# Sliding-window attention scores as row-tiled float32r products: two heads on the two halves of the array

## The chip, the cores and the metric

The kernel runs on one core of one Trainium2 chip. The metric is the device time of one execution in microseconds (us). Three runs of the kernel before gave a median of 2125.07 us. TensorE (PE in the profile) multiplies, VectorE (DVE) and ScalarE (ACT) do the elementwise work, SyncE (SP) issues nearly all transfers. PEld is TensorE's loading of weights, the operand that stays in the array while the other one streams past.

## The reference, cut to what matters

One decoder layer: a projection, four heads of a gated linear recurrence (HGRN2) beside eight heads of sliding-window attention, an output projection, and a gated MLP. Only the scores of the attention are touched by the change:

```python
# q: 8 heads of 64 features; k, v: 2 heads of 64; blocks of 128 queries read
# their own 128 keys and the 128 before them
scale = 1.0 / math.sqrt(ATT_HD)
scores = jnp.einsum('bnqhgd,bnkhd->bnhgqk', qb, kb) * scale
scores = jnp.where(mask, scores, -jnp.inf)          # causal, window of 128
m = jnp.maximum(jnp.max(scores, axis=-1, keepdims=True), sink)
p = jnp.exp(scores - m)
denom = jnp.sum(p, axis=-1, keepdims=True) + jnp.exp(sink - m)
out = jnp.einsum('bnhgqk,bnkhd->bnqhgd', p / denom, vb)
```

## The kernel before, in words

The 2048 tokens are worked through in two halves of 1024. Each half has a mixing stage (projections, recurrence, attention), then the output projection, the MLP with its seven products for a 2x2 block (Strassen's scheme) and the down projection, which also starts the next half.

Nearly every product is made in parts: a float32 operand is split into a high part rounded to float32r (`fp32r` in the profile) and a low part, the rest. A product is then high·high + high·low + low·high, three float32r matmuls into one bank of PSUM.

In the attention a pair `j` (0 to 3) is one head of the first group of four and one of the second, so that its query tile `qT` has 64 features of the one head in rows 0 to 63 and 64 of the other in rows 64 to 127; the keys `kT` have the two key heads in the same way. `rows(kv)` is the half of the rows that belongs to head `kv` of the pair.

`att_keys` (from line 432) makes the keys' tile `KS`, with a column for each of 2 kinds, 128 carried keys and the half's 1024. For head `kv`, `KS[:, kv]` holds the high part of the 64 features in that head's own rows (line 450) and the low part in the other 64 rows (line 451): 128 rows, both parts stacked.

`attend` (from line 463) runs for each pair. For 512 queries (`g`) and each head, lines 479 to 482 make `qh`, the high part of the queries in both halves of the rows, and `ql`, the low part in both halves, by three ACT copies and one DVE subtraction of 64x512 each. Lines 483 to 493 make the scores of two blocks of 128 queries in one PSUM bank `psc`: for each block the matmul with weights `qh` (128 rows, 128 queries) and the moving operand `KS[:, kv]` (128 rows, 256 keys) gives high·high + high·low, the one with `ql` gives low·high + low·low. So two matmuls with all 128 rows give the scores of a head's block: 4 for the two heads of a pair. Over 4 pairs and 16 blocks that is 256. In the first block of the sequence there are only 128 keys. Lines 494 to 502 take the bank to the tile `sc`: an ACT copy of the previous block's half of the scores and a predicated DVE copy of the own block's half.

The banks come from pools of two: `ps("at", ...)` is the pool with which scores (`psc`), transposed probabilities (`ppt`) and attention outputs (`poT`) share two banks; `"hg"` has two for the recurrence, `"mm"` four for the projections.

`ORDER` interleaves the steps of recurrence heads (H) and pairs (A); inside that, a scheduler with its own simulated timeline sets the order of the instructions on each engine when the kernel is built. On PE the score matmuls thus lie in small groups between 128x512 matmuls of the projections (`q`, `g`, `f`, `pop`, `pvv` from line 222 or 750 to 752) and those of the recurrence. PE executes in order.

Some of the recurrence's matmuls and the attention's output have fewer than 128 columns of weights and are put in column tiles: `plev` and `pdiag` (lines 586, 637, 643) in 32 columns, `poT` (line 541) and a last `plev` (line 649) in 64. The profile writes the shape of the weights ahead of the operand: `128*128` is a matmul with all rows and columns, `128*32` and `128*64` are column tiles. A float32 matmul, as in these, stands there as two records, a float32r one as one.

Of the kernel before, what the change touches and what calls it, by code (L numbers as in the profile page):

```python
# [8 lines left out]
F32 = mybir.dt.float32  # L9
F32R = mybir.dt.float32r  # L10
# [3 lines left out]
ALU = mybir.AluOpType  # L14
# [3 lines left out]
P = 128  # L18
# [35 lines left out]
def hymba_layer(ctx: ExitStack, tc: tile.TileContext, a: dict, out: bass.AP):  # L54
    nc = tc.nc
# [18 lines left out]
    def ps(kind, name):  # L74
        return spaces[kind].tile([P, 512], F32, tag=kind, name=name)
# [3 lines left out]
    def halves():  # L79
        return [(b, slice(b * 512, (b + 1) * 512)) for b in range(NB)]  # L80
# [243 lines left out]
    def slot(name):  # L324
        return hp.tile([P, HALF], F32, tag="m", name=name, bufs=KT)
# [103 lines left out]
    def rows(kv):  # L429
        return slice(kv * HD, (kv + 1) * HD)  # L430

    def att_keys(hf, kv, invb, p):

        KS = p.tile([P, 2, P + HALF], F32R, name="KS")
        V = p.tile([P, 1 + TT, P], F32, name="V")
        if hf:
            nc.vector.tensor_copy(KS[:, :, 0:P], kc)  # L440
            nc.vector.tensor_copy(V[:, 0], vc)
        kT, vT = [p.tile([P, HALF], F32, tag="t4", name=n, bufs=2) for n in ("kT", "vT")]
        for jj, dst in ((ATT_J, kT), (ATT_J + 1, vT)):
            o = kv[jj - ATT_J]
            for b, bs in halves():
                nc.vector.tensor_tensor(dst[:, bs], o[b], invb[:, bs], op=ALU.mult)
                nc.scalar.activation(dst[:, bs], dst[:, bs], AF.Identity, bias=C.battn[:, jj:jj + 1])
        for kv in range(2):
            r, other = rows(kv), rows(1 - kv)
            nc.scalar.copy(KS[r, kv, P:], kT[r])  # L450
            nc.vector.tensor_tensor(KS[other, kv, P:], kT[r], KS[r, kv, P:].bitcast(F32), op=ALU.subtract)
        for b in range(NB):
            pv = ps("at", "pv")
            for i in range(4):
                t0 = (b * 4 + i) * P
                nc.tensor.transpose(pv[:, i * P:(i + 1) * P], vT[:, t0:t0 + P], ident)
            nc.scalar.copy(V[:, 1 + 4 * b:5 + 4 * b].rearrange("p a b -> p (a b)"), pv)
        if hf + 1 < NH:
            nc.vector.tensor_copy(kc, KS[:, :, HALF:HALF + P])
            nc.vector.tensor_copy(vc, V[:, TT])  # L460
        return KS, V

    def attend(hf, j, X, invb, KS, V, mix, p):

        o = unit(a["w_att"][j], X, "q")
        qT = slot(f"att{j}")
        for b, bs in halves():
            nc.vector.scalar_tensor_tensor(qT[:, bs], o[b], 0.125, invb[:, bs], op0=ALU.mult, op1=ALU.mult)
            nc.scalar.activation(qT[:, bs], qT[:, bs], AF.Identity, bias=C.bq[:, j:j + 1])
        yield  # L470
        scs = []
        for g in range(NB):
            sc = p.tile([P, 2, 4, P], F32, tag="sc", name="sc", bufs=2)
            gs = slice(g * 512, (g + 1) * 512)
            for kv in range(2):
                r, other = rows(kv), rows(1 - kv)

                qh, ql = [p.tile([P, 512], F32R, tag="pp", name=n, bufs=4) for n in ("qh", "ql")]
                nc.scalar.copy(qh[r], qT[r, gs])
                nc.scalar.copy(qh[other], qT[r, gs])  # L480
                nc.vector.tensor_tensor(ql[r], qT[r, gs], qh[r].bitcast(F32), op=ALU.subtract)
                nc.scalar.copy(ql[other], ql[r].bitcast(F32))
                for i0 in (0, 2):
                    pb = ps("at", "psc")
                    first = hf == 0 and g == 0 and i0 == 0
                    for i in range(2):
                        n = g * 4 + i0 + i
                        w0 = 1 if first and i == 0 else 0
                        o = pb[:, i * 256 + w0 * P:(i + 1) * 256]
                        ks = slice((n + w0) * P, (n + 2) * P)  # L490
                        for t, qx in enumerate((qh, ql)):
                            nc.tensor.matmul(o, qx[:, (i0 + i) * P:(i0 + i + 1) * P], KS[:, kv, ks],
                                             start=t == 0, stop=t == 1)
                    pv = pb.rearrange("p (i w k) -> p i w k", i=2, w=2)
                    dst = sc[:, kv, i0:i0 + 2]
                    if first:
                        nc.vector.memset(dst[:, 0], NEG)
                        nc.scalar.copy(dst[:, 1], pv[:, 1, 0])
                    else:
                        nc.scalar.copy(dst, pv[:, :, 0])  # L500
                    nc.vector.copy_predicated(
                        dst, C.own.bitcast(U32).unsqueeze(1).to_broadcast([P, 2, P]), pv[:, :, 1])
            m = p.tile([P, 2, 4], F32, tag="mx", name="m", bufs=2)
            nc.vector.tensor_reduce(m.rearrange("p a b -> p (a b)"),
                                    sc.rearrange("p a b c -> p (a b) c"), axis=AX.X, op=ALU.max)
            sk = C.sinkb[:, j].unsqueeze(2).to_broadcast([P, 2, 4])
            nc.vector.tensor_tensor(m, m, sk, op=ALU.max)
            es = p.tile([P, 2, 4], F32, tag="es", name="es", bufs=2)
            nc.vector.tensor_tensor(es, sk, m, op=ALU.subtract)
            nc.vector.tensor_scalar(m, m, -1.0, None, op0=ALU.mult)  # L510
            den = p.tile([P, 2, 4], F32, tag="den", name="den", bufs=2)
            for kv in range(2):
                for i in range(4):
                    nc.scalar.activation(sc[:, kv, i], sc[:, kv, i], AF.Exp, bias=m[:, kv, i:i + 1],
                                         accum_out=den[:, kv, i:i + 1])
            nc.scalar.activation(es, es, AF.Exp)
            nc.vector.tensor_tensor(den, den, es, op=ALU.add)
            nc.vector.reciprocal(den, den)
            nc.vector.tensor_tensor(sc, sc, den.unsqueeze(3).to_broadcast([P, 2, 4, P]), op=ALU.mult)
            scs.append(sc)  # L520
        yield
        for g, sc in enumerate(scs):
            pm = []
            for kv in range(2):
                pm.append([p.tile([P, 4, P], F32, tag="pp", name=n, bufs=4) for n in ("po", "pp")])
                pt = ps("at", "ppt")
                for i in range(4):
                    nc.tensor.transpose(pt[:, i * P:(i + 1) * P], sc[:, kv, i], ident)
                ptv = pt.rearrange("p (i q) -> p i q", i=4)
                for dst, mk in zip(pm[kv], (C.ownT, C.prevT)):  # L530
                    nc.vector.tensor_tensor(dst, ptv, mk.unsqueeze(1).to_broadcast([P, 4, P]), op=ALU.mult)
            oT = ps("at", "poT")
            first = None
            for i in (3, 2, 1, 0):
                n = g * 4 + i
                noprev = hf == 0 and n == 0
                for prev in (0,) if noprev else (1, 0):
                    for kv in (1, 0):
                        r = rows(kv)
                        with tc.issue_after(first) if first else ExitStack():  # L540
                            mm = nc.tensor.matmul(oT[r, i * P:(i + 1) * P], V[:, n + 1 - prev, r], pm[kv][prev][:, i],
                                                  start=noprev or prev == 1, stop=prev == 0)
                        first = first or mm.ins
            gs = slice(g * 512, (g + 1) * 512)
            if j < ATT_J - 1:
                nc.scalar.copy(qT[:, gs], oT)
                mix[4 + j] = qT
            else:
                if g == 0:
                    mix[4 + j] = new_x()  # L550
                h, l = mix[4 + j]
                nc.scalar.copy(h[:, gs], oT)
                nc.vector.tensor_tensor(l[:, gs], oT, h[:, gs].bitcast(F32), op=ALU.subtract)
            yield
# [694 lines left out]
    for hf in range(NH):  # L1249
        X, kv, invb, rs, f0 = nxt  # L1250
        with ExitStack() as st:
            p = pool(f"mix{hf}", stack=st, reuse_waits="tile")
            KS, V = att_keys(hf, kv, invb, p)
# [6 lines left out]
            for n, step in enumerate(ORDER.split()):  # L1260
                i = int(step[1:] or 0)
# [16 lines left out]
        with ExitStack() as st:  # L1278
            p = pool(f"ffn{hf}", stack=st, reuse_waits="tile")
            kept, ops, hs, first, last = out_proj(hf, M, p)  # L1280
# [63 lines left out]
```

## Time and profile before

| | |
|---|---|
| median of 3 runs | 2125.07 us (2124.28 to 2125.99) |
| the profiled execution | 2124.22 us |
| its span, first to last instruction | 2122.6 us |
| PE busy | 2108.1 us, 99% of the span |
| DVE, ACT busy | 1624.3 us (77%), 1096.2 us (52%) |
| granted TensorE clock | 1.000 |

A line of the timeline has the start and the duration in us, then engine, line, operation, output<-inputs, the shape of the weights, the shape of the moving operand, and how many such records in a row it merges. Matmuls are pipelined: one record lasts longer than the distance to the next, so the distance from start to start is what a matmul costs in a stream. Scores are made in two stretches, about 114 to 350 us and 1085 to 1400 us of the span.

### The profile page before, as it was taken

What the parts mean: (1) busy time and instruction counts of PE and PEld (TensorE: products, weight loads), DVE (VectorE), ACT (ScalarE), POOL (GpSimd) and SP (SyncE); (2) the same over time, 40 slices, a digit from 0 to 9 for tenths busy, and PEclk for the clock granted to TensorE, in tenths of its full rate; (3) what the DMA queues carried; (4) which work ended last, traced back from release to release, by engine and by line L of the source; (5) the groups of instructions that cost most, each with busy time, mean ns of one, the idle gap of its engine ahead of it and who ended that gap; (6) DMA issues with size and microseconds to landing.
All of it is one profiled execution on the core that took longest, in us unless ns stands there. A gap on an engine that the chain in (4) does not pass through costs nothing.

```text
span 2122.6 us, 29885 instructions
## 1 busy us (share of the span) xinstructions
PE 2108.1 (99%) x11584; PEld 1748.9 (82%) x11584; DVE 1624.3 (77%) x2374; ACT 1096.2 (52%) x1880; POOL 22.3 (1%) x52
## 2 busy tenths in 40 slices
PE   9999999999999999999999999999999999999998
PEld 7888888888888888888888888888888888878888
DVE  7457787898878878775863677868988787887766
ACT  6456575664434444335734476656544444443453
POOL 1000000000000000000000000000000000000000
PEclk9999999999999999999999999999999999999999
DMA  4111111523332325955731010213223223279643
GB/s 160 43 40 43 33 47 47 173 75 101 107 116 85 126 88 190 393 199 168 233 105 52 31 36 31 81 49 142 95 90 124 94 95 119 85 242 372 228 134 134
DMA packets 96475, 255.21 MB, mean 120 GB/s; under 512 B 17355, under 2 KB 19659, under 8 KB 96333
## 3 DMA queue, kind: packets, MB, share of 16 engines
q1 hardware_dynamic: 91076, 251.32, 34.4%
q10 hardware_dynamic: 5256, 1.98, 0.4%
q8 instruction: 91, 1.49, 0.3%
q14 instruction: 52, 0.42, 0.1%
HBM read 195.11 MB, written 57.16 MB: 119 GB/s over the span
## 4 chain that ended last, share of the span: by engine, by line
PE 97%; DVE 1%; ACT 1%; DMA 1%; issue 0%; SPq 0%; DVEq 0%; ACTq 0%
PE pop L222 8%; PE X L933 8%; PE X L934 8%; PE X L935 7%; PE q L222 4%; PE g L222 4%; PE f L222 4%; PE hq L222 4%; PE Y L935 4%; PE Y L933 4%; PE Y L934 4%; PE pdx L1151 3%; PE pdx L1153 3%; PE pdx L1152 3%; PE pdy L1151 3%; PE pdy L1152 3%
## 5 line engine op out<-in xcount | busy, mean ns | idle before, releaser
L758 ACT CAST whi<-raw 128x1024 fp32r<-128x1024 f32 x88 | 92.7, 1053 | 102.9 <-PE X L934 61.1
L933 PE MATMUL X<-T,whi 128*128 128x512 f32 x352 | 137.1, 389 | 0.0
L934 PE MATMUL X<-T,whi 128*128 128x512 f32 x352 | 136.9, 389 | 0.0
L935 PE MATMUL X<-T,wlo 128*128 128x512 f32 x352 | 136.9, 389 | 0.0
L1032 DVE SCALAR_TENSOR_TENSOR y<-ga,cw,y 128x1024 f32<-128x1024 f32 x88 | 112.6, 1281 | 28.4 <-ACT y L1030 28.2
L940 ACT COPY u<-X 128x512 f32<-128x512 f32 x88 | 51.7, 588 | 124.4 <-PE X L935 124.3
L200 ACT CAST whi<-raw 128x1024 fp32r<-128x1024 f32 x57 | 59.5, 1050 | 101.2 <-PE hq L222 33.5
L201 DVE TENSOR_TENSOR wlo<-raw,whi 128x1024 fp32r<-128x1024 f32 x57 | 69.4, 1222 | 54.8 <-ACT whi L200 54.5
L759 DVE TENSOR_TENSOR wlo<-raw,whi 128x1024 fp32r<-128x1024 f32 x88 | 107.4, 1221 | 0.3 <-ACT whi L758 0.3
L222 PE MATMUL pop<-XL,whi 128*128 128x512 f32 x256 | 88.7, 392 | 0.0
L631 ACT COPY G<-QK 128x1024 f32<-128x1024 f32 x48 | 51.4, 1070 | 71.7 <-DVE QK L653 66.5
L222 PE MATMUL pop<-XH,wlo 128*128 128x512 f32 x256 | 88.4, 391 | 0.0
L759 DVE TENSOR_TENSOR xld<-raw,xhd 128x1024 fp32r<-128x1024 f32 x72 | 81.1, 1134 | 9.3 <-ACT xhd L758 9.1
L222 PE MATMUL pop<-XH,whi 128*128 128x512 f32 x256 | 87.9, 394 | 0.0
L758 ACT CAST xhd<-raw 128x1024 fp32r<-128x1024 f32 x72 | 69.6, 978 | 27.1 <-DMA raw<-act0T 7.4
L933 PEld LDWEIGHTS X<-T,whi 128*128 128x128 f32 x352 | 66.1, 188 | 14.1 <-ACT u L940 0.4
L935 PEld LDWEIGHTS X<-T,wlo 128*128 128x128 f32 x352 | 66.1, 188 | 13.8
L934 PEld LDWEIGHTS X<-T,whi 128*128 128x128 f32 x352 | 66.0, 188 | 13.7
L1151 PE MATMUL pdx<-xhd,hid 128*128 128x512 f32 x192 | 74.5, 392 | 1.5 <-ACT xhd L758 0.9
L1152 PE MATMUL pdx<-xld,hid 128*128 128x512 f32 x192 | 74.7, 389 | 0.0
L653 DVE TENSOR_TENSOR QK<-QK,f 128x1024 f32<-128x1024 f32 x56 | 68.6, 1225 | 6.7 <-ACT G L631 5.9
L1153 PE MATMUL pdx<-xhd,lod 128*128 128x512 f32 x192 | 73.7, 389 | 0.0
(394 smaller groups left out, 6329.5 us busy)
## 6 DMA issues: line engine op xcount, KB each, us to landing
wr<-in_w_down SPq DMA_DIRECT2D x90, 512.0 KB, 4.9
raw<-in_w_gate SPq DMA_DIRECT2D x44, 512.0 KB, 3.5
raw<-in_w_up SPq DMA_DIRECT2D x44, 512.0 KB, 3.6
raw<-act0T SPq DMA_DIRECT2D x20, 512.0 KB, 5.0
raw<-act1T SPq DMA_DIRECT2D x20, 512.0 KB, 6.8
act0B<-y SPq DMA_DIRECT2D x33, 256.0 KB, 2.4
act1B<-y SPq DMA_DIRECT2D x33, 256.0 KB, 4.1
raw<-in_w_out SPq DMA_DIRECT2D x16, 512.0 KB, 4.4
```

Source lines behind the costliest of these rows:

```text
L201: nc.vector.tensor_tensor(lo, raw, hi.bitcast(F32), op=ALU.subtract)
L222: marks["unit"] = nc.tensor.matmul(o[b], w, x[:, bs], start=f, stop=l)
L653: done = nc.vector.tensor_tensor(own, own, Fv.rearrange("p b w -> p w b").unsqueeze(3).to_broadcast([P, 2, nb, m]), op=ALU.mult)
L758: return (nc.scalar.copy(h, src), (eng or nc.vector).tensor_tensor(l, src, h.bitcast(F32), op=ALU.subtract))
L759: (eng or nc.vector).tensor_tensor(l, src, h.bitcast(F32), op=ALU.subtract))
L933: nc.tensor.matmul(o, wh[:, ws], xh, start=i == 0 and not more, stop=False, skip_group_check=more)
L934: nc.tensor.matmul(o, wh[:, ws], xl, start=False, stop=False, skip_group_check=more)
L935: r = nc.tensor.matmul(o, wl[:, ws], xh, start=False, stop=i == 3, skip_group_check=more)
L1032: nc.vector.scalar_tensor_tensor(y, g[:, w:w + HALF], C.cw[:, ft, w:w + 1], y, op0=ALU.mult, op1=ALU.add)
L1151: nc.tensor.matmul(o, wh[:, i, c], ah[:, i, cols], start=f, stop=False, skip_group_check=more)
L1152: nc.tensor.matmul(o, wh[:, i, c], al[:, i, cols], start=False, stop=False, skip_group_check=more)
L1153: nc.tensor.matmul(o, wl[:, i, c], ah[:, i, cols], start=False, stop=l, skip_group_check=more)
```

## The change: three products on 64 rows for each head, the heads in turn

`KS` now holds both heads in every column, high parts in `KS[:, 0]` and low parts in `KS[:, 1]`, 64 rows to a head. `qh` and `ql` are the parts of both heads' queries, made by one ACT copy and one DVE subtraction of 128x512. For each block of queries there are three matmuls to a head, `qh`·high, `ql`·high and `qh`·low, each on the 64 rows of that head; in the built program those have a tile of 64 rows and 128 columns, at row 0 for the first head and at row 64 for the second. The code writes the two heads in turn, each into a bank of its own, so that two banks of the pool of two are taken at once. A pair's block has 6 matmuls in place of 4, the whole kernel 384 in place of 256. The product low·low falls away.

```diff
-        for kv in range(2):
-            r, other = rows(kv), rows(1 - kv)
-            nc.scalar.copy(KS[r, kv, P:], kT[r])
-            nc.vector.tensor_tensor(KS[other, kv, P:], kT[r], KS[r, kv, P:].bitcast(F32), op=ALU.subtract)
+        nc.scalar.copy(KS[:, 0, P:], kT)
+        nc.vector.tensor_tensor(KS[:, 1, P:], kT, KS[:, 0, P:].bitcast(F32), op=ALU.subtract)
...
-            for kv in range(2):
-                r, other = rows(kv), rows(1 - kv)
-
-                qh, ql = [p.tile([P, 512], F32R, tag="pp", name=n, bufs=4) for n in ("qh", "ql")]
-                nc.scalar.copy(qh[r], qT[r, gs])
-                nc.scalar.copy(qh[other], qT[r, gs])
-                nc.vector.tensor_tensor(ql[r], qT[r, gs], qh[r].bitcast(F32), op=ALU.subtract)
-                nc.scalar.copy(ql[other], ql[r].bitcast(F32))
-                for i0 in (0, 2):
-                    pb = ps("at", "psc")
...
-                        for t, qx in enumerate((qh, ql)):
-                            nc.tensor.matmul(o, qx[:, (i0 + i) * P:(i0 + i + 1) * P], KS[:, kv, ks],
-                                             start=t == 0, stop=t == 1)
+            qh, ql = [p.tile([P, 512], F32R, tag="pp", name=n, bufs=4) for n in ("qh", "ql")]
+            nc.scalar.copy(qh, qT[:, gs])
+            nc.vector.tensor_tensor(ql, qT[:, gs], qh.bitcast(F32), op=ALU.subtract)
+            for i0 in (0, 2):
+                pbs = [ps("at", "psc") for _ in range(2)]
...
+                    for t, (qx, w) in enumerate(((qh, 0), (ql, 0), (qh, 1))):
+                        for kv in range(2):
+                            r = rows(kv)
+                            nc.tensor.matmul(pbs[kv][:, i * 256 + w0 * P:(i + 1) * 256],
+                                             qx[r, (i0 + i) * P:(i0 + i + 1) * P], KS[r, w, ks], start=t == 0, stop=t == 2)
+                for kv in range(2):
+                    pv = pbs[kv].rearrange("p (i w k) -> p i w k", i=2, w=2)
```

The scheduler orders all of it anew. On PE, in the first half, between the matmuls of a gate's projection (`g0`, `g1` are its two banks), the scores of two blocks of one head stand like this before:

```order
L222 MATMUL g0_1176<-XL_212,whi_1017 128x512
L222 MATMUL g1_1177<-XL_212,whi_1017 128x512
L492 MATMUL psc_1090<-KS_449,qh_1084 128x256
L492 MATMUL psc_1090<-KS_449,ql_1085 128x256
L492 MATMUL psc_1090<-KS_449,qh_1084 128x256
L492 MATMUL psc_1090<-KS_449,ql_1085 128x256
L222 MATMUL g0_1176<-XH_211,wlo_1018 128x512
L222 MATMUL g1_1177<-XH_211,wlo_1018 128x512
```

The other head's bank (`psc_1097`) follows some rows later in the same way. After the change, at the same place, the banks of the two heads are `psc_1086` and `psc_1087`:

```order
L222 MATMUL g0_1174<-XH_228,wlo_1016 128x512
L486 MATMUL psc_1086<-KS_449,qh_1082 128x256
L486 MATMUL psc_1086<-KS_449,ql_1083 128x256
L486 MATMUL psc_1086<-KS_449,qh_1082 128x256 x2
L486 MATMUL psc_1087<-KS_449,qh_1082 128x256
L486 MATMUL psc_1087<-KS_449,ql_1083 128x256
L486 MATMUL psc_1087<-KS_449,qh_1082 128x256 x2
L486 MATMUL psc_1086<-KS_449,ql_1083 128x256
L486 MATMUL psc_1087<-KS_449,ql_1083 128x256
L486 MATMUL psc_1086<-KS_449,qh_1082 128x256
L486 MATMUL psc_1087<-KS_449,qh_1082 128x256
L222 MATMUL g1_1175<-XH_228,wlo_1016 128x512
```

Two runs of four, one for each head's two blocks, have become one run of twelve, in which the two heads are only partly in turn: four of the first, four of the second, then one of each.

A second place on PE is in the second half, among the last products of a recurrence head (`po`). Before, the second head's bank of a group:

```order
L715 MATMUL po_10073<-v_9610,ST_9436 128x128
L492 MATMUL psc_9919<-KS_9253,qh_9906 128x256
L492 MATMUL psc_9919<-KS_9253,ql_9907 128x256
L492 MATMUL psc_9919<-KS_9253,qh_9906 128x256
L492 MATMUL psc_9919<-KS_9253,ql_9907 128x256
L716 MATMUL po_10073<-SS_9959,QK_9433 128x128
```

The first head's four stood some rows earlier, between matmuls of the gate; every neighbour has all 128 rows. After, among the same products:

```order
L711 MATMUL po_10068<-SS_9955,QK_9429 128x128
L486 MATMUL psc_9904<-KS_9251,qh_9882 128x256
L486 MATMUL psc_9904<-KS_9251,ql_9883 128x256
L486 MATMUL psc_9904<-KS_9251,qh_9882 128x256 x2
L486 MATMUL psc_9904<-KS_9251,ql_9883 128x256
L486 MATMUL psc_9904<-KS_9251,qh_9882 128x256
L710 MATMUL po_10068<-v_9606,ST_9432 128x128
L486 MATMUL psc_9905<-KS_9251,qh_9882 128x256
L486 MATMUL psc_9905<-KS_9251,ql_9883 128x256
L486 MATMUL psc_9905<-KS_9251,qh_9882 128x256 x2
L486 MATMUL psc_9905<-KS_9251,ql_9883 128x256
L486 MATMUL psc_9905<-KS_9251,qh_9882 128x256
```

Here all six of one head come first and all six of the other after one matmul with 128 rows, so that no two of them stand in turn.

More of the change, by code (lines that the diff above doesn't have):

```diff
@@ L474, in attend @@
             gs = slice(g * 512, (g + 1) * 512)
-            for kv in range(2):
-                r, other = rows(kv), rows(1 - kv)
-                qh, ql = [p.tile([P, 512], F32R, tag="pp", name=n, bufs=4) for n in ("qh", "ql")]
-                nc.scalar.copy(qh[r], qT[r, gs])
-                nc.scalar.copy(qh[other], qT[r, gs])
-                nc.vector.tensor_tensor(ql[r], qT[r, gs], qh[r].bitcast(F32), op=ALU.subtract)
-                nc.scalar.copy(ql[other], ql[r].bitcast(F32))
-                for i0 in (0, 2):
-                    pb = ps("at", "psc")
[L485 to L490, printed above, removed]
-                        for t, qx in enumerate((qh, ql)):
-                            nc.tensor.matmul(o, qx[:, (i0 + i) * P:(i0 + i + 1) * P], KS[:, kv, ks],
-                                             start=t == 0, stop=t == 1)
-                    pv = pb.rearrange("p (i w k) -> p i w k", i=2, w=2)
+            qh, ql = [p.tile([P, 512], F32R, tag="pp", name=n, bufs=4) for n in ("qh", "ql")]
[3 more added lines that the diff above has]
+                pbs = [ps("at", "psc") for _ in range(2)]
+                first = hf == 0 and g == 0 and i0 == 0
+                for i in range(2):
+                    n = g * 4 + i0 + i
+                    w0 = 1 if first and i == 0 else 0
+                    ks = slice((n + w0) * P, (n + 2) * P)
+                    for t, (qx, w) in enumerate(((qh, 0), (ql, 0), (qh, 1))):
[5 more added lines that the diff above has]
+                    pv = pbs[kv].rearrange("p (i w k) -> p i w k", i=2, w=2)
                     dst = sc[:, kv, i0:i0 + 2]
```

## The prediction

> **What bounds the kernel now.** I read the page first, then the waits of TensorE in the two stretches that make scores, then the timeline around single groups of matmuls.
>
> ```profile
> span 2122.6 us, 29885 instructions
> ...
> PE 2108.1 (99%) x11584; PEld 1748.9 (82%) x11584; DVE 1624.3 (77%) x2374; ACT 1096.2 (52%) x1880; POOL 22.3 (1%) x52
> ...
> PE 97%; DVE 1%; ACT 1%; DMA 1%; issue 0%; SPq 0%; DVEq 0%; ACTq 0%
> ```
>
> These are the span, the busy times, and the shares of the chain that ended last: 97% of the chain is PE. PE's waits from 60 to 360 us and from 1085 to 1425 us of the span (who waited, for whom, us, times, longest) are one row each:
>
> ```profile
> PE po L715 <- DVE SS L701: 0.4, 1, 0.4
> ...
> PE poT L541 <- DVE y L180: 0.9, 1, 0.9
> ```
>
> So where scores are made PE waits 1.3 us in all. The change is costed as PE's own time, start to start; lighter ACT and DVE work can give back 1.3 us at most. The scores before are 256 matmuls, with all 128 rows:
>
> ```profile
> L492 PE MATMUL psc<-KS,qh x128: 220/282/389, 114.2 to 1397.3; 128*128 128x256 f32 x120, 128*128 128x128 f32 x8
> ...
> L492 PE MATMUL psc<-KS,ql x128: 273/282/389, 114.2 to 1397.5; 128*128 128x256 f32 x120, 128*128 128x128 f32 x8
> ...
> 114.64 0.28 PE L492 MATMUL psc<-KS,qh 128*128 128x256 f32 x1
> 114.76 0.28 PE L492 MATMUL psc<-KS,ql 128*128 128x256 f32 x1
> 114.88 0.28 PE L492 MATMUL psc<-KS,qh 128*128 128x256 f32 x1
> 115.00 0.28 PE L492 MATMUL psc<-KS,ql 128*128 128x256 f32 x1
> ```
>
> Though one lasts 0.28 us, the next starts 0.12 us later. That is the price of a score matmul of 256 keys, and I call it a slot.
>
> **The change, part by part.** *The stream.* The change makes 384 matmuls of 256 slots' work. They cost less only if the two heads' tiles run beside each other. No matmul with 64 rows is in this trace. The nearest rows are column tiles, all rows but 32 or 64 columns (a stretch of the timeline with two of them, and the durations of all of that form):
>
> ```profile
> 148.02 0.28 PE L541 MATMUL poT<-po,V 128*64 128x128 f32 x2
> ...
> L541 PE MATMUL poT<-po,V x256: 272/273/273, 148.0 to 1413.7; 128*64 128x128 f32 x128
> ```
>
> Two `poT` matmuls of 0.273 us take 0.28 us together: tiles in different columns overlap almost wholly. I take the same for tiles in different rows: a matmul of the other head right behind costs nothing, one of the same head costs a slot. The order then counts, since PE issues in order. In the built order after the change, the 384 stand in 46 unbroken runs: 22 have all twelve of a group, 14 of these strictly in turn (6 slots), 5 with a doubled start (7), 3 worse (9, 9, 11). Seven runs are six matmuls of one head alone, as at the second place in the order shown above: 6 slots for half the work. The other 17 are shorter pieces. All runs together are 238 slots. Before there were 256, so the stream gains 18 x 0.12 = 2.2 us, where strict turns throughout would have gained (256 − 192) x 0.12 = 7.7 us. (16 matmuls before and 24 after are half as wide; I leave that out.)
>
> [...]
>
> *The changes of shape.* What a change between all columns and column tiles costs, the timeline shows, with the weight loads behind:
>
> ```profile
> 71.93 0.39 PE L750 MATMUL pvv<-whi,XH 128*128 128x512 f32 x1
> 72.15 0.39 PE L751 MATMUL pvv<-whi,XL 128*128 128x512 f32 x1
> 72.47 0.76 PE L643 MATMUL plev<-G 128*32 128x32 f32 x64
> ...
> 73.04 0.20 PE L643 MATMUL plev<-G 128*32 128x32 f32 x1
> 73.17 0.51 PE L752 MATMUL pvv<-wlo,XH 128*128 128x512 f32 x1
> 73.51 0.39 PE L750 MATMUL pvv<-whi,XH 128*128 128x512 f32 x1
> 73.73 0.39 PE L751 MATMUL pvv<-whi,XL 128*128 128x512 f32 x1
> ...
> 73.16 0.19 PEld L752 LDWEIGHTS pvv<-wlo,XH 128*128 128x128 f32 x1
> 73.27 0.19 PEld L750 LDWEIGHTS pvv<-whi,XH 128*128 128x128 f32 x1
> ```
>
> From one 128x512 matmul to the next it is 0.22 to 0.23 us. Into the tiles (72.15 to 72.47) it is 0.32: 0.095 too much. Out of them, the last `plev` at 73.04 is followed after 0.13 us, where 32 columns are a matter of 0.03: again 0.095. Then the matmul behind the first full one comes after 0.34 instead of 0.23: 0.11 more, because the first weights (73.16) were not loaded ahead. The second load starts 0.11 behind the first: that is how long a load of 128 columns holds its path. So going back to the full array costs 0.095 + 0.11 = 0.205 us, and going into 32-column tiles about 0.11 with their shorter first load. The 113 changes of shape that I count in the built order all look like this in the trace where nothing else waits.
>
> Score matmuls before had all rows and columns and caused no change of shape: in the rows of 114.64 us and on, nothing of the kind stands. After, each of the 46 runs is a change into row tiles and one out. Counted in the two orders:
>
> - into the full array 52 before, 68 after: 16 x 0.205 = +3.3 us
> - into row tiles 0 before, 46 after. Their weights have all 128 columns, so I take 0.095 and a first load as for the full array, 0.105, the two tiles' loads side by side: 46 x 0.20 = +9.2 us. Lower end 0.095 alone, 4.4 us; upper end two loads in turn, 0.31, 14.3 us
> - into column tiles 61 before, 58 after: 3 x 0.11 = −0.3 us
>
> That a change to row tiles drains like one to column tiles is the step that this trace does not show. [...]
>
> *Copies.* Casts and subtractions on ACT and DVE get fewer:
>
> ```profile
> L479 ACT CAST qh<-att x32: 597/617/623, 71.1 to 1380.4; 64x512 fp32r<-64x512 f32 x32
> L481 DVE TENSOR_TENSOR ql<-att,qh x32: 671/686/690, 73.0 to 1381.3; 64x512 fp32r<-64x512 f32 x32
> L450 ACT CAST KS<-kT x4: 1032/1038/1046, 43.0 to 1091.0; 64x1024 fp32r<-64x1024 f32 x4
> ```
>
> Three ACT lines of 32 casts at 0.617 us become 16: 80 x 0.617 = 49 us off ACT; DVE loses 16 x 0.686 = 11 us; the keys' split loses half. PE waits for none of it beyond the 1.3 us above, so I put the gain at nothing, and 1.3 us at the best end.
>
> *The two banks at once.* A group now needs both banks of its pool, so the first matmul of the next group waits until two evacuations are over, with all of PE's queue behind it (gate projections, `po`) and the softmax behind that. An evacuation is a copy and a predicated copy:
>
> ```profile
> L500 ACT COPY sc<-psc x56: 345/372/393, 116.5 to 1397.8; 128x256 f32<-128x256 f32 x56
> L501 DVE COPY_PREDICATED sc<-own,psc x64: 391/444/457, 115.3 to 1398.2; 128x256 f32<-128x256 uint32 x64
> ```
>
> Two are 2 x (0.372 + 0.444) = 1.6 us even if nothing overlaps. In the built order the least that PE has between two of the 32 groups is seven 128x512 matmuls and 32 `plev`: 7 x 0.22 = 1.5 us for the seven, and the `plev`'s two changes of shape, 0.11 + 0.205, make 1.8. That hides it; uncovered it would be up to 1.6 us a group. I take 0.
>
> *The sum.* −2.2 + 3.3 + 9.2 − 0.3 = +10.0 us. The profiled execution took 2124.22 us (span 2122.6), so it would take 2134.2; it lies 0.85 under the median of the runs, 2125.07, and on the median's scale I forecast **2135.1 us**. Ends of this case: with 4.4 for the entries and the 1.3 of waits gone, +3.9, 2129.0; with 14.3, +15.1, 2140.2.
>
> **The rivals.**
>
> *Row tiles do not overlap.* If they run one after another, the stream is 384 slots, +15.4 us in place of −2.2, so +27.6 in all: 2152.7. If only their weight loads take turns at 0.11 each, it is 384 x 0.11 − 256 x 0.12 = +11.5, so +23.7: 2148.8. For it: two tiles in different rows use the same 128 columns, of which no row here shows two users. Against it: column tiles overlap in loading and in streaming. [...]
>
> *Row tiles are free to enter (not slower).* If the array keeps its set-up when only rows are split, the 46 entries cost nothing, and changes to and from column tiles are fewer by three each way: −3 x (0.205 + 0.11) = −0.9, with the stream −2.2: −3.1, 2122.0. It decides where a run costs less than 0.16 us in all: −3.1 + 46 x 0.16 = 4.25. For it: loads are shaped by columns, and columns stay at 128. Against it: 32 to 64 columns, both split, pays 0.095 too.
>
> *Faster.* The same, and the lighter ACT and DVE take all of PE's 1.3 us of waits away: −4.4, 2120.7.
>
> *The change doesn't do what it says:* the heads are not in turn where the scheduler says so. This is counted already in the 238 slots.
>
> **How the numbers follow.** A measurement of this kernel tells about 0.2%, 4.25 us, from no change. My forecast (drain at each run, tiles overlap) has 0.68; no overlap 0.16; free entry 0.12; faster 0.04. The range from 2129 to 2153 holds the forecast's ends and both forms of no overlap, and leaves out 0.16. Slower by over 0.2% (above 2129.3): 0.68 + 0.16 less 0.02 for the forecast's low end, 0.82. Within 0.2%: 0.12 + 0.02 = 0.14. Faster: 0.04.
>
> **What would show it.** In the profile after, `psc` rows have `64*128`; two matmuls of different heads start some ns apart and the next pair 0.12 us later; the gap ahead of a run is 0.095 us more than the stream needs, its second pair is 0.105 late, and the return costs 0.205. Single-head runs of six go at 0.12 each. Pairs 0.22 to 0.24 apart would be the first rival; a run entered without a gap the second. A PE wait for DVE or ACT at the start of a run would break the argument on the two banks.

## The result, and the profile after

The changed kernel takes 2135.22 us, the median of 6 runs (2133.01 to 2136.75); the kernel before, run beside it, 2124.98 us (2123.93 to 2125.99, 6 runs). The ratio is 1.0048, with a 95% interval from 1.0038 to 1.0059: slower by 10.2 us. The forecast was 2135.1. That the two agree within 0.1 us is in part luck: as shown below, two terms of the sum were off by 1 to 2 us each, in opposite directions.

The page of the changed kernel, the lines that were shown of before (the shares of the chain by engine last):

```profile
span 2133.4 us, 30028 instructions
...
PE 2117.3 (99%) x11712; PEld 1748.3 (82%) x11712; DVE 1610.8 (76%) x2356; ACT 1036.0 (49%) x1792; POOL 20.9 (1%) x52
...
PE 96%; DMA 1%; DVE 1%; ACT 1%; issue 0%; SPq 0%; DVEq 0%; ACTq 0%
```

PE is still the bound, and the span is 10.8 us longer. ACT lost 60 us of work and DVE 13.5, which shows nowhere in the time. The records rose by 128, the additional score matmuls. Their group in the profile (durations: least, median, most):

```profile
L486 PEld LDWEIGHTS psc<-KS,qh x256: 182/184/189, 115.9 to 1405.7; 64*128 64x128 f32 x128
L486 PE MATMUL psc<-KS,qh x256: 270/278/386, 115.9 to 1405.8; 64*128 64x256 f32 x120, 64*128 64x128 f32 x8
...
L486 PE MATMUL psc<-KS,ql x128: 271/278/386, 116.0 to 1405.7; 64*128 64x256 f32 x120, 64*128 64x128 f32 x8
```

The shape of the weights is `64*128`, and a matmul on 64 rows lasts as long as one on 128 did (0.278 against 0.282 us), as does its weight load (0.184 against 0.188). All gain must come from overlap. The timeline of PE at the first of the two places whose order is shown ahead of the prediction, the run of twelve between `g0` and `g1`:

```profile
126.99 0.39 PE L222 MATMUL g<-XH,wlo 128*128 128x512 f32 x1
127.31 0.40 PE L486 MATMUL psc<-KS,qh 64*128 64x256 f32 x2
127.53 0.29 PE L486 MATMUL psc<-KS,ql 64*128 64x256 f32 x2
127.65 0.41 PE L486 MATMUL psc<-KS,qh 64*128 64x256 f32 x4
127.88 0.29 PE L486 MATMUL psc<-KS,ql 64*128 64x256 f32 x2
128.00 0.29 PE L486 MATMUL psc<-KS,qh 64*128 64x256 f32 x2
128.22 0.50 PE L222 MATMUL g<-XH,wlo 128*128 128x512 f32 x1
128.56 0.62 PE L222 MATMUL g<-XH,whi 128*128 128x512 f32 x2
```

Read from the top: into the run it is 0.32 us instead of 0.227, so 0.09 of gap; two matmuls together last 0.29 us where one lasts 0.278, so the heads do overlap; the second pair comes 0.22 behind the first and the later ones 0.12, so the first weight load costs 0.10; out of the run it is again 0.22 where 0.12 was due; and the second full matmul is 0.34 behind the first, the load of 0.11 more. The weight loads in the same stretch, two at a time:

```profile
127.31 0.20 PEld L486 LDWEIGHTS psc<-KS,qh 64*128 64x128 f32 x2 [0.35 <-DVE SS L696]
127.42 0.20 PEld L486 LDWEIGHTS psc<-KS,ql 64*128 64x128 f32 x2
127.53 0.20 PEld L486 LDWEIGHTS psc<-KS,qh 64*128 64x128 f32 x2
```

Two loads take 0.20 us together, one 0.184: they are side by side as well.

And the waits. Of PE's longest, this one was not there before:

```profile
PE psc L486 <- DVE sc L496: 2.0, 4, 1.1
...
PE kv L391 <- ACT XH L380: 1.6, 2, 0.9
```

PE waits 2.0 us, in four places, for the predicated copy that frees a bank of scores. Other waits got shorter: in the two mixing stages all of PE's waits together are 3.1 us, and were 2.2 (the 1.3 of the prediction leave out one of 0.9 just behind its window). (The second row lies in the first 12 us, ahead of anything that was changed, and differs from run to run.)

Not all of the 10.8 us lies where the change is. From the first matmul of `pvv` to the first one of the MLP (`X`), a mixing stage and the output projection took 358.2 us in the first half and 358.7 in the second; after the change they take 359.7 and 366.1, together 8.8 us more. Another 1.6 us lie ahead of the first `pvv`. There the changed kernel's profiled execution has a stretch at half the granted clock, and the one of before has none (the stretch, its length, busy time and instructions of PE, PEld, DVE, ACT and POOL, the granted clock, the busy share of DMA and GB/s; the changed kernel first, then before):

```profile
10.90:14.40 3.50, 3.50 (x8) 2.79 (x9) 3.11 (x5) 3.42 (x4) 0.00 (x0) 0.51 1.04 424
```

```profile
10.90:14.40 3.50, 3.50 (x15) 2.87 (x16) 3.18 (x5) 3.50 (x4) 0.00 (x0) 1.00 1.03 417
```

PE is busy throughout in both and starts 8 matmuls in place of 15. Nothing that was changed runs there, so this is not the change's doing; how much of it the medians hold, the record does not show.

### The profile page after: what moved, and what is told of

Same layout as the page of the kernel before. It is cut to its first block, busy times and chain, and to the rows that moved or that the text cites. A ratio compares the mean times of both kernels' runs of the same rounds, so it can differ in the third digit from the quotient of the medians.

```text
span 2133.4 us, 30028 instructions
## 1 busy us (share of the span) xinstructions
PE 2117.3 (99%) x11712; PEld 1748.3 (82%) x11712; DVE 1610.8 (76%) x2356; ACT 1036.0 (49%) x1792; POOL 20.9 (1%) x52
## 4 chain that ended last, share of the span: by engine, by line
PE 96%; DMA 1%; DVE 1%; ACT 1%; issue 0%; SPq 0%; DVEq 0%; ACTq 0%
PE pop L222 8%; PE X L928 7%; PE X L929 7%; PE X L930 7%; PE hq L222 4%; PE q L222 4%; PE f L222 4%; PE Y L929 4%; PE Y L928 4%; PE Y L930 4%; PE g L222 4%; PE pdx L1146 3%; PE pdx L1147 3%; PE pdx L1148 3%; PE pdy L1147 3%; PE pdy L1146 3%
```

## The experiments

Three explanations stood against each other. Mine: changes of shape on PE cost what the sum took, tiles of rows overlap, and the difference of the two is the slowdown. The first rival: the changes are free, and more matmuls, in tiles that hardly overlap, make it slower. The second: it is the two banks taken together. Ratios are to the kernel before, measured on the same chip: its median there was 2124.53 us for the version with priority and for the two banks without row tiles, 2124.31 for the other versions up to the first runs of 24, and 2124.76 for the rest. Differences from the changed kernel's 2135.22 us join medians of separate measurements, and so carry up to 0.7 us of these.

**Cutting each run in two.** A matmul of two columns on the full array between the two blocks of a group; its columns are overwritten by the scores that follow. The chain (`issue_after`) also keeps the twelve in the order in which they are written.

```diff
+                    if i:
+                        with tc.issue_after(last):
+                            last = nc.tensor.matmul(pbs[0][:, 256:258], ones_r, ones_r[:, 0:2], start=True, stop=True).ins
...
+                            with tc.issue_after(last) if last else ExitStack():
```

> The changed kernel, with one small matmul on the full array (2 columns, overwritten afterwards) between the two blocks of each of the 32 groups, so that nearly each run of row tiles is cut in two. The built order has 255 changes of shape in place of 172: 42 more into the full array, 41 more into row tiles. Theory (changes of shape cost what the sum took, 0.205 and 0.20 us each): 42 x 0.205 + 41 x 0.20 = +16.8 us, a little less for runs that need fewer slots, so 2150 to 2153 us. Rival (changes to row tiles are free, the 128 additional matmuls or the two banks taken at once made the kernel slower): 32 small matmuls with their weight loads, 32 x 0.12 = +3.8 us, 2139 us.

Measured: 2144.48 us (2143.94 to 2145.18), ratio to before 1.0093 (1.0079 to 1.0107). That is 9.3 us above the changed kernel: two and a half times what the rival allows, and some 6 us less than the theory said. One cut in the timeline of PE:

```profile
121.52 0.39 PE L491 MATMUL psc<-KS,qh 64*128 64x256 f32 x2
121.84 0.27 PE L486 MATMUL psc<-ones_r 128*128 128x2 f32 x1
122.04 0.39 PE L491 MATMUL psc<-KS,qh 64*128 64x256 f32 x2
122.26 0.28 PE L491 MATMUL psc<-KS,ql 64*128 64x256 f32 x2
122.38 0.29 PE L491 MATMUL psc<-KS,qh 64*128 64x256 f32 x2
```

The last start ahead of the cut is 121.63 (the second of the x2 row). From there to 122.04 is 0.41 instead of 0.12, and the pair behind comes after 0.22 instead of 0.12: one change to the full array and one back cost 0.39 us, as the sum has it (0.205 + 0.20). The trace has 87 runs of row tiles where the changed kernel's has 46, as was expected. What is missing to the expected size is elsewhere. More of the matmuls start in pairs: counting starts less than 40 ns apart as one, there are 211 and not 230, which is 19 x 0.12 = 2.3 us. And PE's waits in the mixing stages are 0.7 us and not 3.1. 16.8 − 2.3 − 2.4 = 12.1 us, and the mixing stages of this trace are 11.6 us longer than those of the changed kernel's. So the price holds in the trace. The medians differ by less, 9.3 us, and so do the spans, since the key projections at the start of the two halves (`kv`) take 2.6 us less here, counted start to start; 1.7 of that is the stretch at half clock shown above, which this execution does not have.

**Three products without tiles.** The query tile of a head has zeros in the other head's 64 rows.

```diff
+            for kv in range(2):
+                r, other = rows(kv), rows(1 - kv)
+                qh, ql = [p.tile([P, 512], F32R, tag="pp", name=n, bufs=4) for n in ("qh", "ql")]
+                for x in (qh, ql):
+                    nc.gpsimd.memset(x[other].bitcast(F32), 0.0)
...
+                                             qx[:, (i0 + i) * P:(i0 + i + 1) * P], KS[:, w, ks], start=t == 0, stop=t == 2)
```

> The same three products and the same banks as in the change, but every score matmul has all 128 rows: the query tile of a head has zeros in the other head's rows, so there are 384 matmuls on the full array and no change of shape for them (106 in all, 7 fewer than before). Theory: 384 - 256 = 128 slots more x 0.12 = +15.4, less 7 changes, about -1.2: +14 us on before, 2139 us; so row tiles overlap and save some 20 us of stream, and their changes of shape take some 18 of it away again. Rival (row tiles do not overlap, their changes are free): the same 384 slots as the change has, no slower than it, 2135 or below. Rival (two banks at once are what costs): this kernel pays for the banks and for 128 matmuls, about 2150.

Measured: 2138.34 us (2137.96 to 2138.93), 1.0065 (1.0049 to 1.008): +14.0 us, as the theory had it. Without overlap and with free changes of shape it would have been no slower than the changed kernel; it is slower by 3.1. (It takes two banks together as well, but in its trace no wait of PE is put down to the copies that empty them.) Two matmuls one after another, in its timeline, take 0.40 us where two row tiles took 0.29:

```profile
115.12 0.40 PE L492 MATMUL psc<-KS,ql 128*128 128x256 f32 x2
115.36 0.40 PE L492 MATMUL psc<-KS,qh 128*128 128x256 f32 x2
```

So tiles of rows are worth about as much as their changes of shape cost, and only 3 to 5 us of their gain is left (3.1 between the medians, 5.2 between the mixing stages of the two traces).

**Fewer runs.** Only the order of products and heads in the code: the first matmul of a group now needs its last operand.

```diff
-                    for t, (qx, w) in enumerate(((qh, 0), (ql, 0), (qh, 1))):
-                        for kv in range(2):
+                    for t, (qx, w) in enumerate(((ql, 0), (qh, 0), (qh, 1))):
+                        for kv in (1, 0):
```

> The changed kernel with the low queries' product first and the second head ahead of the first, so that a group starts only when its last operand and its last bank are there: 39 runs of row tiles in place of 46, 161 changes of shape in place of 172. Theory: 4 fewer into the full array x 0.205, 7 fewer into row tiles x 0.20, and 8 slots fewer x 0.12: -3.2 us on the change, 2132 us. Rival (number of matmuls or the two banks decide): those stay as they are, 2135 us.

Measured: 2131.0 us (2128.87 to 2131.88), 1.0029 (1.0017 to 1.004). That is 4.2 below the changed kernel, with the same matmuls and the same banks, and with PE's waits as long in all (9.9 us, and 10.0 in the changed kernel's trace): the number of matmuls does not decide, that of runs counts. The size is less sure than the medians make it look: the mixing stages of the two traces differ by 2.4 us, where 3.2 were expected, and 1.7 us of the difference of the spans is the stretch at half clock.

**The same with priority** in the scheduler for the score matmuls (`with tc.high_priority():` around them, in the order of products and heads of the version just shown).

> The changed kernel with the low queries' product first, the second head first, and the score matmuls with priority in the scheduler: 36 runs, 158 changes of shape (7 more into the full array than before the change, 36 into row tiles, 2 more into column tiles), 216 slots. Theory: 7 x 0.205 + 36 x 0.20 + 0.2 - 40 x 0.12 = +4 us on before, 2129 us. If the number of matmuls decides, 2135 us. It is the one version with two banks to a group that comes nearest to the kernel before; by the theory it does not pass it.

Measured: 2129.88 us (2128.89 to 2132.17), 1.0026 (1.0016 to 1.0035). Expected were 2129. (The starts in its trace make 238 groups, though, where 216 slots were expected.) It is the best version with row tiles, and still slower than the kernel before.

**Runs of 24.** All four blocks of 512 queries in one group, in four banks.

```diff
+            banks = [[ps(kind, "psc") for _ in range(2)] for kind in ("at", "mm")]
...
+                for i0, pbs in zip((0, 2), banks):
+                    for i in range(2):
```

> As the one before, and a group is all four blocks of 512 queries, 24 matmuls, into four banks: two of the scores' pool and two of the projections' pool. The built order has 21 runs of row tiles and 125 changes of shape: 8 fewer into the full array than before the change, 21 more into row tiles, 1 fewer into column tiles. Theory: -8 x 0.205 + 21 x 0.20 - 0.1, and 196 slots in place of 256, -60 x 0.12 = -7.1: -4.5 us on before, 2120.5 us, if taking two banks from the projections makes PE wait nowhere. Rival (waits for banks taken together): four at once make it worse, above 2135. Rival (number of matmuls): 2135.

Measured: 2177.57 us (2177.35 to 2177.73), 1.0248 (1.0234 to 1.0262). The shapes were as few as expected; the condition "if taking two banks from the projections makes PE wait nowhere" did not hold. With priority for the groups:

> Groups of 24 in four banks as before, but their matmuls have priority in the scheduler, so that they stand as early as their operands are there: 23 runs, 138 changes of shape. By shapes and slots alone -1 us on before, 2123 us. If what held up the first version of it was the place that the scheduler gave the groups, this should be near that. If four banks taken together are what holds up, it stays tens of us above, 2150 us or more.

Measured: 2177.48 us (2176.95 to 2177.82), 1.0248 (1.0233 to 1.0263). The place of the groups in the queue was not it. The kernel before with the same four banks, its matmuls untouched:

```diff
+            banks = [[ps(kind, "psc") for _ in range(2)] for kind in ("at", "mm")]
...
-                    pb = ps("at", "psc")
+                    pb = banks[i0 // 2][kv]
```

> The kernel before, its matmuls and copies as they are, but the scores of 512 queries and both heads go into four banks taken together, two of the scores' pool and two of the projections' pool. It asks what made the groups of 24 slow. If four banks taken together hold up the queues: slower by some tens of us here too, above 2150 us. If it was the row tiles in large runs: 118 changes of shape in place of 113, about +1 us, 2125 to 2126 us.

Measured: 2188.23 us (2187.32 to 2189.45), 1.0299 (1.0284 to 1.0314): worse than with row tiles. So four banks taken together held up the mixing stage with either shape of the matmuls, `64*128` (2177.57 us) and `128*128` (2188.23). PE's waits in this kernel, the longest:

```profile
PE plev L644 <- DVE strip L617: 14.3, 4, 4.2
PE psc L493 <- ACT qh L481: 7.2, 11, 1.1
PE psc L493 <- DVE sc L502: 4.2, 2, 2.8
```

PE's waits are 44.9 us in all, and 8.4 before. The recurrence (`plev`) waits longest, 14.3 us for DVE's `strip`; the score matmuls (`psc`) wait 12.6 us for their queries and their banks, and projections 2.5 us for a bank that scores still hold. The waits are not the whole. In seven stretches of the mixing stages, 61 us together, the granted clock of this trace is 0.50; PE is busy for 49.7 us of them, and by estimate half of that, 25 us, is the price of the clock: at 0.51, in the stretch of the changed kernel shown above, PE started 8 matmuls where before it started 15. The waits' 36.5 us and these 25 are nearly all of the 63.5. The same shows in the first kernel with runs of 24, where a slot that takes 0.12 us at full clock takes 0.22 in such a stretch (0.50 from 1257.6 to 1264.4 us):

```profile
1261.50 0.41 PE L486 MATMUL psc<-KS,ql 64*128 64x256 f32 x2
1261.72 0.62 PE L486 MATMUL psc<-KS,qh 64*128 64x256 f32 x4
```

How the four banks bring DVE behind, by the scheduler's order or by the projections' missing banks, and whether the waits bring the clock down, these runs do not tell.

**Two banks together, without row tiles.** The kernel before, with the two heads' banks taken as in the change; the query tiles of both heads are now made ahead of their matmuls.

```diff
+            for i0 in (0, 2):
+                pbs = [ps("at", "psc") for _ in range(2)]
+                for kv in range(2):
+                    pb = pbs[kv]
...
+                        for t, qx in enumerate(qs[kv]):
```

> The kernel before, all matmuls on the full array, but the two heads' banks of a group are taken together, as in the change. 114 changes of shape, 256 slots: by shapes and slots +0.1 us. If taking the two banks together makes PE wait as in the change's trace (2.0 us for the predicated copies): about +2 us, 2127 us. If the waits come with the row tiles' order only: 2125 us.

Measured: 2127.33 us (2126.37 to 2128.56), 1.0013 (1.0004 to 1.0021), so +2.8 us, with 0.9 to 4.5 in the interval. Taking the banks in pairs cost something by itself here. How it does is less clear than the expectation had it: PE's waits in the mixing stages are 4.4 us, 2.2 more than before, but only 0.8 of them is for a bank of scores. In any case it is a part of the change's 10, not the whole, as the second rival would have it.

**The copies put back.**

```diff
+            for kv in range(2):
+                r, other = rows(kv), rows(1 - kv)
+                for _ in range(3 - kv):
+                    nc.scalar.copy(qh[r], qT[r, gs])
+            nc.vector.tensor_tensor(ql[r], qT[r, gs], qh[r].bitcast(F32), op=ALU.subtract)
```

> The changed kernel with the copies put back that it saves: for each 512 queries five ACT copies of 64x512 and one DVE subtraction of 64x512 are done again to no use. The built order moves a little: 170 changes of shape, 40 runs. If lighter ACT and DVE gave the change nothing: by shapes and slots 2 more into the full array, 6 fewer runs, 7 fewer slots, some 1 to 1.5 us below the change, 2134 us. If they hid part of the cost: above it, 2137 us or more.

Measured: 2134.06 us (2133.75 to 2136.42), 1.0043 (1.0026 to 1.006). No slower than the change, and as expected if the copies are worth nothing: the 49 us taken off ACT gave nothing back that the scatter of these executions, 2 to 3 us, would let one see.

**Head after head.** The six matmuls of one head are written and chained ahead of the six of the other.

```diff
+                with tc.high_priority():
...
+                    todo = [(i, t, kv) for i in range(2) for t in range(3) for kv in range(2)]
+                    todo.sort(key=lambda x: (x[2], x[0], x[1]))
+                    for i, t, kv in todo:
...
+                        with tc.issue_after(last) if last else ExitStack():
```

> The changed kernel with the six matmuls of one head written and chained ahead of the six of the other, early in PE's queue: 17 unbroken runs of twelve, 30 of six, 182 changes of shape. The forecast took the matmuls to start strictly in the order of the queue: then such a run of twelve takes 11 slots, 1.4 us from its first start to its last. If each head's tile goes at its own pace as far as PE looks ahead, fewer: 9 slots, about 1.05 us, as the one such run of the changed kernel's trace. By that, 69 into the full array, 47 runs: some 2145 us, by strict order some 3 us more.

One execution: 2149.75 us. That is nearer to what was expected of strict order, but PE's score matmuls wait 5.0 us for DVE in its trace, 3.0 more than in the changed kernel's, so the time alone decides nothing. The starts do. A run of six matmuls of the one head queued ahead of six of the other, on PE's timeline:

```profile
338.40 0.38 PE L490 MATMUL psc<-KS,ql 64*128 64x256 f32 x1
338.62 0.39 PE L490 MATMUL psc<-KS,qh 64*128 64x256 f32 x2
338.75 0.39 PE L490 MATMUL psc<-KS,ql 64*128 64x256 f32 x2
338.97 0.40 PE L490 MATMUL psc<-KS,qh 64*128 64x256 f32 x4
339.20 0.28 PE L490 MATMUL psc<-KS,ql 64*128 64x256 f32 x1
339.32 0.40 PE L490 MATMUL psc<-KS,qh 64*128 64x256 f32 x2
339.65 0.50 PE L222 MATMUL pop<-XH,wlo 128*128 128x512 f32 x1
```

From the first start to the last it is 1.04 us (339.44 less 338.40): 9 slots with the first load, not 11. 13 of the 17 such runs of this trace take 1.042 to 1.048 us; the other four, one for each pair, have the sequence's first block with its 128 keys and take 0.96. The second head's first matmul, seventh in the queue, started with the first head's third, while the fourth to sixth still waited. So for row tiles strict order is wrong, in the prediction and in the words "PE executes in order" ahead of it. What the trace of before shows is matmuls on all rows that start in the built order, at both places whose order is shown ahead of the prediction (rows from 123.20 to 124.21 us and from 1183.25 to 1183.84).

## Why the prediction was right, point by point

*PE alone sets the time, and lighter ACT and DVE are worth nothing:* right. The copies put back changed nothing that can be seen.

*A run pays for going in and coming out:* right, in mechanism and size. Into row tiles the forecast had 0.095 + 0.105, the trace shows 0.09 + 0.10; back to the full array 0.205, the trace 0.09 to 0.10 + 0.11. A cut costs 0.39 where 0.405 was forecast. That going into row tiles has the gap of going into column tiles, 0.095 us, was the author's estimate, which the trace of before couldn't show; the changed kernel's trace shows 0.09. The three versions that differ in the number of runs agree: 2135.2 with 46 runs, 2131.0 with 39, 2129.9 with 36. In their traces the two mixing stages take 725.8, 723.4 and 722.5 us, and 717.0 before.

*Row tiles overlap, in streaming and loading:* right. Pairs take 0.29 us, with starts 0 to 18 ns apart, and two loads 0.20.

*The stream gains 18 slots, 2.2 us:* this step was mis-sized. It took PE to start matmuls in the order of the queue, and counted 238 slots. In the traces each head's tile goes at its own pace within a run: the run shown first, queued as four, four, then in turn, was counted as 9 slots and took 6 pairs. Counted so, the changed kernel's runs are 222 slots. In the trace their starts make 230 groups, some of them split off only because PE waited for a bank. So the gain is 26 to 34 slots, 3.1 to 4.1 us, 1 to 2 us more than forecast.

*Two banks at once are hidden:* this was the other mis-sized step. I put them at 0, since 1.8 us of PE work lies between two groups and two evacuations take 1.6. PE waits 2.0 us for these banks. Since other waits got shorter, the net is 0.9 us in the mixing stages (3.1 for 2.2). The prediction had named the sign, a wait for DVE at the start of a run. The longest of the four waits, 1.1 us, in the second half, DVE first and PE behind it:

```profile
1311.75 0.30 DVE L614 COPY_PREDICATED strip<-lmask,odd 126x64 f32<-126x64 uint32 x1 [1.30 <-DMA odd<-moved]
1311.89 1.22 DVE L648 TENSOR_TENSOR QK<-QK,f 128x1024 f32<-128x1024 f32 x1
1313.03 0.77 DVE L496 COPY_PREDICATED sc<-own,psc 128x256 f32<-128x256 uint32 x2
```

```profile
1313.52 0.38 PE L486 MATMUL psc<-KS,qh 64*128 64x256 f32 x1 [1.08 <-DVE sc L496]
```

The evacuations are as short as forecast (0.77 for two). They stand in DVE's queue behind a predicated copy of the recurrence that waits 1.30 us for a transfer, and a product of 1.22 us. The cover was measured in PE's work; it had to be measured in DVE's queue.

*The sum:* 3.3 + 9.2 − 0.3 as forecast, −3.1 to −4.1 for −2.2, +0.9 for 0: +9.0 to +10.0 us. The mixing stages of the two traces differ by 8.8. So the mechanism is right and its sizes hold within about 1 us, but the agreement of the total is better than the terms deserve: the two errors cancel, and 1.6 us of the spans' difference is the stretch at half clock, of which the forecast knew nothing.

*The rivals:* no overlap (2149 to 2153) and free entry (2122) both fall by the first run shown.

## What to carry to other kernels

In this kernel a small product on part of the array paid for two changes of shape, 0.4 us for a run between full matmuls. Two row tiles saved one slot of 0.12 us for every pair, six in a run of twelve, and the third product took four of them back; the two left, 0.24 us, didn't pay for 0.4. Before splitting the array, count the runs in the built order, not the matmuls. When two banks are taken together, look for cover in the queue of the engine that empties them: here 1.30 us of waiting for a transfer and a product of 1.22 us, ahead of the copies in that queue, reached PE as its longest wait for a bank, 1.1 us. And compare two traces stage by stage, with the granted clock beside it, before a difference of 1 or 2 us is given to a term of the sum.

## What the runs showed of the hardware that was not expected

Matmuls in different row tiles did not start strictly in the order of the queue. In the run of four and four the fifth, of the other tile, started 13 ns behind the first, ahead of three of the first tile; in those of six and six the seventh started 7 ns behind the third, again ahead of three.

A matmul with half the rows saved nothing alone: it lasted 0.278 us against 0.282 for 128 rows, its start lay 0.12 from the next as theirs did, and its weights loaded in 0.184 us against 0.188.

With PE busy, the granted clock fell to half in single stretches of some us: once in the changed kernel's profiled execution, for 3.4 us from 10.95 us on, and for 61 us in all, in seven stretches, in the kernel before with four banks, where they are by estimate 25 of the 63.5 us lost. The mean granted clock of that execution, 0.985, hardly tells.
